# Up-projection of a gated feed-forward block by one level of Strassen's algorithm, with the down-projection as a stage of its own

## The chip, the core and the metric

The kernel runs on one core of a Trainium2 chip. The core has a matrix engine (TensorE, PE in the rows; PEld is its weight load), VectorE (DVE), ScalarE (ACT), GpSimd (POOL), and a queue engine SyncE (SP) that issues most transfers. Matmuls accumulate into eight PSUM banks; everything else lives in SBUF or, outside the core, in DRAM. The metric is the device time of one execution in microseconds, lower is better.

## What is computed

One decoder block on 1024 tokens of width 1024: two mixers (retention and sparse attention), a merge, an output projection, then a convolutional feed-forward block and a last norm. The change touches what follows the merge:

```python
x = x + merged @ w_out[l]
x = x + conv_ffn(rmsnorm(x, norm_ffn[l]), w_up[l], conv_w[l], conv_b[l], w_down[l])
...
def conv_ffn(h, w_up, conv_w, conv_b, w_down):
    a, b = jnp.split(h @ w_up, 2, axis=-1)          # w_up: 1024 x 5632
    a_pad = jnp.pad(a, ((0, 0), (CONV_W - 1, 0), (0, 0)))
    ac = conv_b + sum(conv_w[i] * a_pad[:, i:i + S] for i in range(CONV_W))
    return (jax.nn.gelu(ac) * b) @ w_down           # w_down: 2816 x 1024
```

All of it is wanted to float32 accuracy.

## The kernel before

**Split arithmetic.** Every operand of a matmul is kept as two tiles in the reduced float format that TensorE takes: `split` (line 128) writes the high part by a ScalarE copy and the low part by a VectorE subtraction that reads the high part. `mm3` (line 132) then makes three matmuls: high by high, high by low, low by high. One accumulation over 1024 input rows is 8 x 3 matmuls of 128 x 128 weights and 512 moving columns.

**Order.** Nobody wrote the order of the engines' instructions out by hand: the tile framework takes the program text as priority and a scheduler orders each engine's instructions. Every engine then runs its list strictly in that order, a transfer issue included, which waits in its engine's list like any other instruction. Tiles come from pools with a fixed number of buffers per tag: `wraw` (3, raw weights), `wsp` (4 per tag, `wh` and `wl`), `big` (4 of 16 KB per partition, tag `A`), `mpool` (12 of 8 KB, tag `B`), `fpool` (small rows). A new tile waits until the last reader of the buffer's former tile is done.

**Output projection** (from line 802). For each 512-column half `ch` and each token tile `t` of 128, eight k steps of `mm3` fill a bank `ps_mm`, and VectorE adds it to the residual row `x1[t]`, which stays in SBUF to the end. In the second half each tile is also normalised (`rms_row`: squares on ScalarE, power on GpSimd, scaling on VectorE), transposed by TensorE (eight 128 x 128 transposes) and split into `h2`, the moving operand of the up-projection (`hF`). Tiles go in the order 0 to 7.

**Up and down** (`up`, `down_weights`, `down`, from line 865). Features are taken in blocks `f` of 128. For a block and a token half `hf`, `up` makes two accumulations (the a and the b column block) of 24 matmuls, then ScalarE and VectorE do the convolution over tokens, Gelu, product and split; the gated rows `g2` stay in SBUF. Every two blocks `down` multiplies them by two rows of blocks of `w_down` and VectorE adds the sums to `x1`. Up of one pair and down of the pair before it alternate, and at the end the rows are normalised and stored.

Of the kernel before, what the change touches and what calls it, by code (L numbers as in the profile page):

```python
# [18 lines left out]
P = 128  # L19
# [65 lines left out]
def tile_hybrid_block(ctx: ExitStack, tc: tile.TileContext, x, norm_mix, w_in, ret_gn_g,  # L85
# [46 lines left out]
    def mm3(ps, ah, al, bh, bl, start, stop):  # L132
        nc.tensor.matmul(ps, ah, bh, start=start, stop=False)  # L133
        nc.tensor.matmul(ps, ah, bl, start=False, stop=False)  # L134
        return nc.tensor.matmul(ps, al, bh, start=False, stop=stop)  # L135
# [663 lines left out]

    x1 = [wsp.tile([P, D], F32, name=f"x1_{t}", tag="wh" if t < 4 else "wl") for t in range(NT)]  # L800
    hF = {}
    fpool = ctx.enter_context(tc.tile_pool(name="ftmp", bufs=1))
    gf = fpool.tile([P, D], F32, name="gf", tag="gain")
    nc.sync.dma_start(gf, bcast(norm_ffn[0], D))
    wo1 = [big.tile([P, KD, 512], F32R, name=f"wo1{i}", tag="A") for i in range(2)]

    def rms_row(t, gain, dst=None):
        hx = fpool.tile([P, D], F32, name="hx", tag="ft", bufs=3)
        ss = fpool.tile([P, 3], F32, name="ss", bufs=2)
        for i in range(2):  # L810
            c = slice(i * 512, i * 512 + 512)
            nc.scalar.activation(hx[:, c], x1[t][:, c], AF.Square, accum_out=ss[:, i:i + 1])
# [3 lines left out]
        for i in range(2):  # L816
            c = slice(i * 512, i * 512 + 512)
            nc.vector.scalar_tensor_tensor(hx[:, c], x1[t][:, c], r, gain[:, c],
# [4 lines left out]

    for t in range(NT):
        nc.sync.dma_start(x1[t], x[t * P:(t + 1) * P, :])
    for ch in range(2):
        cs = slice(ch * 512, ch * 512 + 512)
        for t in range(NT):
# [12 lines left out]
            if j == 0:  # L841
                hq = [half_quad("h2") for _ in range(2)]
                for k in range(KD):
                    hF[k, hf] = tuple(q[:, k % 4, :] for q in hq[k // 4])
            hx = rms_row(t, gf)
            for i in range(2):
# [4 lines left out]
                split(hq[i][0][:, :, c], hq[i][1][:, :, c], pt)  # L851
# [10 lines left out]
    wu, arow, g2, wd = {}, {}, {}, {}  # L862

    def up(f, hf):

        if hf == 0:
            wt = big.tile([P, 2, 2, KD, P], F32R, name="wu", tag="A")
            for i, c0 in ((0, f * P), (1, DFF + f * P)):
                raw = wraw.tile([P, KD, P], F32, name="wu_raw", tag="raw")
                nc.sync.dma_start(raw, w_up[:, c0:c0 + P].rearrange("(k p) c -> p k c", p=P))  # L870
                wu[f, i] = (wt[:, i, 0], wt[:, i, 1])
                split(*wu[f, i], raw)
        ps = []
        for i in range(2):
# [52 lines left out]
    for f in range(0, NF, 2):  # L927
        fs = (f, f + 1)
        for i in fs:
            up(i, 0)  # L930
# [34 lines left out]
```

## Time and profile before

| | us |
|---|---|
| median of 3 runs (1823.77 to 4637.19) | 1824.64 |
| the profiled execution | 1826.17 |
| its span, first to last instruction | 1824.4 |
| TensorE busy in it | 1791.2 (98%) |
| VectorE / ScalarE / GpSimd busy | 994.0 / 716.8 / 87.5 |
| weight loads busy (beside matmuls) | 1528.3 (84%) |

The profile counts an engine as busy while one of its instructions runs; a matmul's duration overlaps the next one's, so that the step from start to start, not the duration, says how fast they go. "Idle before" is the time in which an engine waited ahead of an instruction, with what ended the wait behind the arrow. The granted clock is the share of TensorE's full clock (1.00 is the upper of its two levels, 2.4 GHz, 0.50 the lower, 1.2 GHz); over the whole span it is 0.996.

### The profile page before, as it was taken

Reading aid. Unit: us, or ns where it says so; the run is one execution under the profiler, and the core shown is the slowest. Engines: PE = TensorE matmul, PEld = TensorE weight load, DVE = VectorE, ACT = ScalarE, POOL = GpSimd, SP = SyncE. Lnnn points to the kernel's source line nnn. Section 1 sums busy time; section 2 is a strip of 40 time slices with the busy share of each in tenths; the row PEclk is TensorE's granted clock in tenths of the full one; section 3 lists DMA queues with packets and bytes.
Section 4 is the critical chain, followed back from the end, with each engine's and each line's share of the span. In section 5 each row is a group of like instructions: output and inputs, shape, how many; then the busy total and the mean of one; then the engine's idle time right before and its main releaser. Section 6 shows DMA issues by size and latency. Waiting matters only on the chain.

```text
span 1824.4 us, 24239 instructions
## 1 busy us (share of the span) xinstructions
PE 1791.2 (98%) x9401; PEld 1528.3 (84%) x9401; DVE 994.0 (54%) x2245; ACT 716.8 (39%) x1345; POOL 87.5 (5%) x94
## 2 busy tenths in 40 slices
PE   8999999999999999999998999999999999999998
PEld 7888888988889988989777888888888888888886
DVE  6537666666667835557354355454344444445346
ACT  5435555554556734445443234122122222222213
POOL 1000000000000011220022000000000000000000
PEclk9999999999999999999999999999999999999999
DMA  5342222122221252223676303121121021112002
GB/s 204 110 142 70 73 62 72 50 80 65 63 80 53 68 154 85 70 87 129 219 235 227 120 1 98 30 70 35 35 70 47 24 69 58 35 47 70 12 1 93
DMA packets 164003, 151.08 MB, mean 83 GB/s; under 512 B 7606, under 2 KB 137134, under 8 KB 163886
## 3 DMA queue, kind: packets, MB, share of 16 engines
q1 hardware_dynamic: 142926, 122.77, 22.2%
q10 hardware_dynamic: 20960, 26.75, 4.1%
q8 instruction: 74, 1.21, 0.3%
q14 instruction: 43, 0.35, 0.1%
HBM read 118.55 MB, written 30.93 MB: 82 GB/s over the span
## 4 chain that ended last, share of the span: by engine, by line
PE 88%; DMA 5%; DVE 3%; ACT 2%; issue 1%; POOL 0%; SPq 0%; DVEq 0%; ACTq 0%; POOLq 0%
PE ps_mm L133 16%; PE ps_mm L134 16%; PE ps_mm L135 16%; PE ps_sc L133 7%; PE ps_sc L134 7%; PE ps_sc L135 7%; PE ps_pt L509 3%; PE ps_pv L134 2%; PE ps_pv L133 2%; PE ps_pv L135 2%; PE ps_sc L396 2%; PE ps_sc L395 2%; PE ps_pv L516 2%; PE ps_pv L515 2%; DMA sga<-ga_scr 1%
## 5 line engine op out<-in xcount | busy, mean ns | idle before, releaser
L133 PE MATMUL ps_sc<-h2h,wu 128*128 128x512 f32 x528 | 205.7, 390 | 0.0
L135 PE MATMUL ps_sc<-h2h,wu 128*128 128x512 f32 x528 | 205.4, 389 | 0.0
L134 PE MATMUL ps_sc<-h2l,wu 128*128 128x512 f32 x528 | 205.4, 389 | 0.0
L133 PE MATMUL ps_mm<-hTh,w_hi 128*128 128x512 f32 x512 | 202.1, 395 | 2.4 <-DVE ql L130 2.0
L134 PE MATMUL ps_mm<-hTl,w_hi 128*128 128x512 f32 x512 | 201.9, 394 | 0.0
L135 PE MATMUL ps_mm<-hTh,w_lo 128*128 128x512 f32 x512 | 201.1, 393 | 0.0
L922 DVE TENSOR_TENSOR x<-ps_mm,x 128x512 f32<-128x512 f32 x176 | 120.6, 690 | 146.4 <-PE ps_mm L135 144.8
L133 PE MATMUL ps_mm<-w_hi,hTh 128*128 128x256 f32 (+1 forms) x576 | 167.0, 290 | 1.7 <-DVE kl L130 1.1
L135 PE MATMUL ps_mm<-w_hi,hTl 128*128 128x256 f32 (+1 forms) x576 | 167.2, 290 | 0.0
L134 PE MATMUL ps_mm<-w_lo,hTh 128*128 128x256 f32 (+1 forms) x576 | 166.8, 290 | 0.0
L130 DVE TENSOR_TENSOR w_lo<-w_raw,w_hi 128x1024 fp32r<-128x1024 f32 (+2 forms) x75 | 92.0, 1229 | 110.4 <-ACT w_hi L129 110.4
L133 PE MATMUL ps_mm<-wd,g 128*128 128x512 f32 x352 | 137.5, 391 | 0.7 <-DVE ms L156 0.7
L134 PE MATMUL ps_mm<-wd,g 128*128 128x512 f32 x352 | 137.0, 389 | 0.0
L135 PE MATMUL ps_mm<-wd,g 128*128 128x512 f32 x352 | 137.0, 389 | 0.0
L129 ACT ACTIVATE pth<-ps_pt 128x512 fp32r<-128x512 f32 x132 | 76.6, 593 | 107.3 <-PE ps_pt L509 106.4
L133 PEld LDWEIGHTS ps_sc<-h2h,wu 128*128 128x128 f32 x528 | 99.1, 188 | 20.6
L135 PEld LDWEIGHTS ps_sc<-h2h,wu 128*128 128x128 f32 x528 | 99.0, 188 | 20.6
L134 PEld LDWEIGHTS ps_sc<-h2l,wu 128*128 128x128 f32 x528 | 99.1, 188 | 20.4
L133 PEld LDWEIGHTS ps_mm<-hTh,w_hi 128*128 128x128 f32 x512 | 96.3, 188 | 22.0 <-DVE ql L130 2.4
L133 PEld LDWEIGHTS ps_mm<-w_hi,hTh 128*128 128x128 f32 x576 | 110.5, 192 | 3.4 <-DVE kl L130 1.3
L135 PEld LDWEIGHTS ps_mm<-hTh,w_lo 128*128 128x128 f32 x512 | 96.3, 188 | 18.8 <-DVE w_lo L130 0.3
L134 PEld LDWEIGHTS ps_mm<-hTl,w_hi 128*128 128x128 f32 x512 | 96.3, 188 | 18.1
(284 smaller groups left out, 3782.9 us busy)
## 6 DMA issues: line engine op xcount, KB each, us to landing
w_raw<-in_w_in SPq DMA_DIRECT2D x48, 512.0 KB, 3.9
wu_raw<-in_w_up SPq DMA_DIRECT2D x44, 512.0 KB, 3.8
wd_raw<-in_w_down SPq DMA_DIRECT2D x22, 512.0 KB, 3.5
xt<-in_x SPq DMA_DIRECT2D x8, 512.0 KB, 5.2
qr<-q_scr SPq DMA_DIRECT2D x64, 64.0 KB, 2.4
ga_scr<-ge ACTq DMA_DIRECT2D x16, 256.0 KB, 2.0
rg_scr<-ge ACTq DMA_DIRECT2D x16, 256.0 KB, 2.1
gb_scr<-ge ACTq DMA_DIRECT2D x16, 256.0 KB, 2.0
```

Of the source, the lines that this page charges most:

```text
L129: nc.scalar.activation(hi, src, AF.Copy)
L130: nc.vector.tensor_sub(lo, src, f32(hi))
L133: nc.tensor.matmul(ps, ah, bh, start=start, stop=False)
L134: nc.tensor.matmul(ps, ah, bl, start=False, stop=False)
L135: return nc.tensor.matmul(ps, al, bh, start=False, stop=stop)
L395: nc.tensor.matmul(dst, q1[:, r, :], kap, start=True, stop=False)
L396: nc.tensor.matmul(dst, q2[:, r, :], kap, start=False, stop=True)
L509: nc.tensor.transpose(pt[:, r, :], pr[r][:, kt * P:(kt + 1) * P], ident)
L515: nc.tensor.matmul(pv[0:DK], v[:, 0:DK], ptl, start=False, stop=False)
L516: nc.tensor.matmul(pv, v, pth, start=False, stop=last)
L922: nc.vector.tensor_add(x1[t][:, cs], ps, x1[t][:, cs])
```

## The change

The up-projection is done on 2 x 2 blocks with seven products in place of eight (Strassen's algorithm in Winograd's form). The normalised input is cut into token halves and input halves (a11, a12 for tokens 0 to 511, a21, a22 for the others; the second index is the half of the 1024 inputs), and a 256-column strip of `w_up` into b11 to b22 (first index: input half, second: 128-column block). The sums s1 = a21 + a22, s2 = s1 - a11, s3 = a11 - a21 and s4 = a12 - s2 are made once, on the fly, as tiles are normalised; for that the second half of the output projection takes tiles 4 to 7 first, then 0 to 3. For every strip the differences t1 = b12 - b11, t2 = b22 - t1, t3 = b22 - b12 and t4 = b21 - t2 are made by VectorE and split too. `seven` makes the seven products of one strip (4 k steps, 12 matmuls each) in three banks: `c` collects s1 t1 and then s4 b22, `xb` collects a11 b11, s2 t2, s3 t3 and a22 t4, `yb` holds a12 b21. Between two products into one bank the partial sum is copied out (`kept`) or read by the output step; `skip_group_check` only allows accumulation to go on after a read. The last product (a22 t4) of a strip is put off into the next strip.

The a strip of two blocks is followed by their b strip. Outputs are rows of 1024 tokens in the one buffer `rows`; the convolution works on 1024 tokens at a time. The gated rows go to DRAM (`g_scr`, 44 writes of 256 KB issued by ScalarE). x1 goes to DRAM as well (`x1_scr`) and its buffers are used for weights. Behind the whole up stage the down stage loads x1, the gated rows (22 loads of 512 KB) and `w_down`, splits both, and accumulates two, then five times four feature blocks per bank. The last norm is interleaved with the last chunk.

```diff
-        for t in range(NT):
+        for t in (range(NT) if ch == 0 else (4, 5, 6, 7, 0, 1, 2, 3)):
...
+            hx = rms_row(t, x1[t], gf)
+            nc.scalar.dma_start(x1_scr[t], x1[t])
...
-                split(hq[i][0][:, :, c], hq[i][1][:, :, c], pt)
+                if hf == 1:
+                    if i == 0:
+                        nc.scalar.activation(fa[:, 0, :, c], pt, AF.Copy)
+                    else:
+                        split(a22[0][:, :, c], a22[1][:, :, c], pt)
+                        nc.vector.tensor_add(fa[:, 1, :, c], pt, fa[:, 0, :, c])
+                        split(s1[0][:, :, c], s1[1][:, :, c], fa[:, 1, :, c])
+                elif i == 0:
+                    split(a11[0][:, :, c], a11[1][:, :, c], pt)
+                    nc.vector.tensor_sub(fa[:, 0, :, c], pt, fa[:, 0, :, c])
+                    nc.vector.tensor_sub(fa[:, 1, :, c], fa[:, 1, :, c], pt)
+                else:
+                    split(a12[0][:, :, c], a12[1][:, :, c], pt)
+                    nc.vector.tensor_sub(fb[:, :, c], pt, fa[:, 1, :, c])
...
+        nc.vector.tensor_sub(t12[:, 0], b12, b11)
+        nc.vector.tensor_sub(t12[:, 1], b22, t12[:, 0])
+        split(wt[:, 0, 0:2], wt[:, 1, 0:2], t12)
...
+    def product(ps, a, b, start, stop):
+        for k in range(4):
+            mm3(ps, b[0][:, k, :], b[1][:, k, :], a[0][:, k, :], a[1][:, k, :],
+                start and k == 0, stop and k == 3, not start)
...
+        c = bank("sc")
+        product(c, s1, t1, True, True)
+        m5 = kept(c, 0)
+        xb = bank("mm")
+        product(xb, a11, b11, True, True)
+        m1 = kept(xb, 1)
+        while late:
+            late.pop()()
+        yb = bank("pt")
+        product(yb, a12, b21, True, True)
+        out(0, yb, m1)
+        product(xb, s2, t2, False, True)
+        u2 = kept(xb, 1)
+        product(c, s4, b22, False, True)
+        out(1, c, u2)
+        product(xb, s3, t3, False, True)
+        out(3, xb, m5)
+        def last():
+            product(xb, a22, t4, False, True)
+            out(2, xb, None)
+        late.append(last)
...
+                nc.vector.tensor_add(in1, in0, in1)
+                nc.vector.tensor_mul(g, in1, g)
+            nc.scalar.dma_start(g_scr[f + i % 2][:, tok], g)
...
+            ws[f] = rows_split(f, "wd", w_down[f * P:(f + 1) * P, :], *(
+                (big, "A") if f < 2 else (mpool, "B")))
+            gs[f] = rows_split(f, "g", g_scr[f], *(
+                (big, "A") if f < 2 or f % 4 < 2 else (mpool, "B")))
```

The built orders at three places. First TensorE at the end of the output projection, before: `ps_mm` is the last token tile (7), `wo` and `m` its operands, `ps_sc` the first up-projection accumulation, of tokens 0 to 511.

```order
L134 MATMUL ps_mm_11199<-wo11_10601,mh_10252 128x512
L135 MATMUL ps_mm_11199<-wo10_10600,ml_10253 128x512
L133 MATMUL ps_sc_11268<-h2h_10860,wu_11259 128x512
L134 MATMUL ps_sc_11268<-h2l_10861,wu_11259 128x512
L135 MATMUL ps_sc_11268<-h2h_10860,wu_11259 128x512
```

The same place in the changed kernel: `ps_mm_11255` is token tile 3, the last one now; the L865 rows are the transposes of tiles 2 (`hx_11226`) and 3 (`hx_11281`); `ps_mm_11374` and `ps_mm_11484` are the a11 products of the first and the second strip.

```order
L135 MATMUL ps_mm_11255<-wo10_10600,ml_10251 128x512
L865 MATMUL ps_pt_11238<-ident_116,hx_11226 128x128 x4
L865 MATMUL ps_pt_11247<-ident_116,hx_11226 128x128 x4
L865 MATMUL ps_pt_11293<-ident_116,hx_11281 128x128 x4
L865 MATMUL ps_pt_11302<-ident_116,hx_11281 128x128 x4
L133 MATMUL ps_mm_11374<-a11h_11112,d11_11346 128x512
L133 MATMUL ps_mm_11484<-a11h_11112,d11_11456 128x512
L134 MATMUL ps_mm_11374<-a11l_11113,d11_11346 128x512
```

The first product moved behind the transposes of the last tile; before, products of the first token half stood directly behind the output projection, with the transposes of later tiles among them.

Second, VectorE at the norm of tile 3. Before, from the residual sum of tile 3 to that of tile 4:

```order
L835 TENSOR_TENSOR x1_3_10590<-ps_mm_10991,x1_3_10590 128x512
L813 TENSOR_TENSOR ss_11018<-ss_11018 128x1
L156 TENSOR_SCALAR ms_11023<-ss_11018 128x1
L818 SCALAR_TENSOR_TENSOR hx_11017<-x1_3_10590,r_11022,gf_10598 128x512 x2
L130 TENSOR_TENSOR h2l_10861<-ps_pt_10977,h2h_10860 128x4x128
L130 TENSOR_TENSOR h2l_10863<-ps_pt_10984,h2h_10862 128x4x128
L835 TENSOR_TENSOR x1_4_10591<-ps_mm_11042,x1_4_10591 128x512
```

In the changed kernel, from the small sum of squares of tile 3 (its residual sum stands six rows ahead, with `fb`, `t12`, `a11l` and two `fa` rows between) to the low part of a11 for this tile (`a11l` from `ps_pt_11293`):

```order
L821 TENSOR_TENSOR ss_11282<-ss_11282 128x1
L920 TENSOR_TENSOR t34_11340<-wu_raw_11337,wu_raw_11335 128x512
L921 TENSOR_TENSOR t34_11340<-wu_raw_11337,t12_11339 128x512
L130 TENSOR_TENSOR a12l_11115<-ps_pt_11247,a12h_11114 128x4x128
L881 TENSOR_TENSOR fb_10895<-ps_pt_11247,fa_10894 128x4x128
L156 TENSOR_SCALAR ms_11287<-ss_11282 128x1
L826 SCALAR_TENSOR_TENSOR hx_11281<-x1_3_10590,r_11286,gf_10598 128x512 x2
L130 TENSOR_TENSOR d21_11459<-wu_raw_11447,d21_11459 128x512
L130 TENSOR_TENSOR d22_11466<-wu_raw_11447,d22_11466 128x512
L130 TENSOR_TENSOR d11_11585<-wu_raw_11574,d11_11585 128x512
L130 TENSOR_TENSOR a11l_11113<-ps_pt_11293,a11h_11112 128x4x128
```

Between the norm's steps stand differences for the strips (`t34`), the a12 and s4 rows of tile 2 and the splits of plain weight blocks (`d21`, `d22`, `d11`).

Third, ScalarE near the end of the up stage. Before, around the last blocks: convolution (L890), Gelu (L896), gated rows (`g2`) and evictions (L882), with the splits of `w_down` among them.

```order
L882 ACTIVATE ar_15387<-ps_sc_15337 128x512
L890 ACTIVATE ac_15392<-ps_sc_15337,cw_11250 128x512
L129 ACTIVATE wd_15466<-wd_raw_15464 128x1024
L129 ACTIVATE wd_15471<-wd_raw_15469 128x1024
L896 ACTIVATE ac_15392<-ac_15392 128x512
L129 ACTIVATE g2_15325<-ac_15392 128x512
```

In the changed kernel, from the last output of the last a strip (L979) on: `wd` and `g` are tiles of the down stage, L989 and L995 the scaled copy and Gelu of the last pair, `m_13999` the u2 copy of the last strip.

```order
L979 ACTIVATE rows_11334<-ps_mm_13890 128x512
L129 ACTIVATE wd_14138<-wd_raw_14136 128x1024
L989 ACTIVATE rows_11334<-rows_11334,cw_11327 128x1024
L129 ACTIVATE g_14143<-g_raw_14141 128x1024
L995 ACTIVATE rows_11334<-rows_11334 128x1024
L1005 DMA g_scr20_10630<-rows_11334 128x512
L946 ACTIVATE m_13999<-ps_mm_14014 128x512
L129 ACTIVATE wd_14286<-wd_raw_14284 128x1024
L1005 DMA g_scr21_10631<-rows_11334 128x512 x2
L129 ACTIVATE g_14291<-g_raw_14289 128x1024
L129 ACTIVATE wd_14148<-wd_raw_14146 128x1024
L1005 DMA g_scr20_10630<-rows_11334 128x512
```

The split of the first gated row read back (`g_14143`) now stands between the scaled copy and the Gelu of the last pair, and the second one's weights and rows stand behind the last writes to `g_scr`.

## Rows read from the trace of the kernel before

**Rows 1.** Windows: us; busy (count) of PE, PEld, DVE, ACT, POOL; clock, DMA, GB/s.

```profile
1041.00:1094.60 53.60, 53.60 (x263) 44.82 (x262) 26.38 (x51) 15.46 (x38) 3.83 (x7) 1.00 0.08 24
1094.60:1798.00 703.40, 703.40 (x3113) 582.56 (x3112) 317.44 (x477) 177.43 (x249) 0.55 (x1) 1.00 0.15 45
```

**Rows 2.** Who waited, PE, 1040 to the end: us, times, longest.

```profile
PE ps_mm L133 <- DVE ms L156: 0.7, 1, 0.7
```

**Rows 3.** Timeline of PE: start us, us; the first and the twelfth after it.

```profile
1797.83 0.39 PE L133 MATMUL ps_mm<-wd,g 128*128 128x512 f32 x1
...
1800.55 0.39 PE L133 MATMUL ps_mm<-wd,g 128*128 128x512 f32 x1
```

**Rows 4.** Tiles h2h and wd: count, ns min/median/max, first and last start.

```profile
L133 PEld LDWEIGHTS ps_sc<-h2h,wu x528: 187/188/190, 1094.6 to 1786.7; 128*128 128x128 f32 x176
L135 PE MATMUL ps_mm<-wd,g x352: 387/389/397, 1140.7 to 1816.4; 128*128 128x512 f32 x176
```

**Rows 5.** Groups by shape, DVE: count, busy us, mean ns, idle before.

```profile
L130 DVE TENSOR_TENSOR wu<-wu_raw,wu 128x1024 fp32r<-128x1024 f32 x44 | 53.9, 1225 | 75.6 <-ACT wu L129 75.6
...
L130 DVE TENSOR_TENSOR g<-ac,g 128x512 fp32r<-128x512 f32 x44 | 30.2, 686 | 1.4 <-ACT g L129 1.4
...
L207 DVE SCALAR_TENSOR_TENSOR hx<-xt,r,gm 128x1024 f32<-128x1024 f32 x8 | 10.2, 1281 | 1.4 <-POOL r L157 1.4
```

**Rows 6.** Groups by shape, ACT.

```profile
L129 ACT ACTIVATE wu<-wu_raw 128x1024 fp32r<-128x1024 f32 x44 | 46.7, 1061 | 140.7 <-DMA wu_raw<-in_w_up 130.2 <-PE ps_mm L135 6.9 <-PE ps_sc L135 1.9
...
L890 ACT ACTIVATE ac<-ps_sc,cw 128x512 f32<-128x512 f32 x44 | 34.0, 774 | 0.0
...
L882 ACT ACTIVATE ar<-ps_sc 128x512 f32<-128x512 f32 x44 | 26.3, 599 | 179.4 <-PE ps_sc L135 179.2
```

**Rows 7.** DMA issues of the page: count, KB, us to landing.

```profile
wu_raw<-in_w_up SPq DMA_DIRECT2D x44, 512.0 KB, 3.8
...
ga_scr<-ge ACTq DMA_DIRECT2D x16, 256.0 KB, 2.0
```

**Rows 8.** Timeline of DVE, norm of tile 7 behind the output projection.

```profile
1097.00 0.15 DVE L813 TENSOR_TENSOR ss<-ss 128x1 f32<-128x1 f32 x1
1097.19 0.15 DVE L156 TENSOR_SCALAR ms<-ss 128x1 f32<-128x1 f32 x1
1098.07 1.41 DVE L818 SCALAR_TENSOR_TENSOR hx<-x,r,gf 128x512 f32<-128x512 f32 x2 [0.73 <-POOL r L157]
1099.40 1.28 DVE L130 TENSOR_TENSOR h2l<-ps_pt,h2h 128x512 fp32r<-128x512 f32 x2
```

**Rows 9.** Timeline of PE, transposes of one normalised tile.

```profile
1058.99 1.04 PE L849 MATMUL ps_pt<-ident,hx 128*128 128x128 f32 x8
```

**Rows 10.** Timeline of PE behind two holes.

```profile
875.75 0.50 PE L133 MATMUL ps_mm<-oh,w_hi 128*128 128x512 f32 x1 [1.97 <-ACT yb L595]
...
1004.42 0.80 PE L133 MATMUL ps_mm<-woh,mh 128*128 128x512 f32 x1 [4.69 <-ACT mh L129]
...
1006.72 0.63 PE L133 MATMUL ps_mm<-woh,mh 128*128 128x512 f32 x1
1007.15 0.63 PE L134 MATMUL ps_mm<-wol,mh 128*128 128x512 f32 x1
...
1010.43 0.40 PE L133 MATMUL ps_mm<-woh,mh 128*128 128x512 f32 x1
```

**Rows 11.** Windows of 2 us behind those holes.

```profile
876.00:878.00 2.00, 2.00 (x8) 1.59 (x8) 1.69 (x2) 1.21 (x2) 0.00 (x0) 0.79 0.62 196
878.00:880.00 2.00, 2.00 (x6) 1.54 (x6) 1.22 (x1) 0.97 (x2) 0.00 (x0) 0.50 0.89 265
880.00:882.00 2.00, 2.00 (x9) 1.65 (x8) 0.16 (x1) 1.25 (x2) 0.00 (x0) 0.86 0.80 254
...
1008.00:1010.00 2.00, 2.00 (x6) 1.61 (x5) 2.00 (x3) 0.72 (x2) 0.00 (x0) 0.50 0.21 68
```

More of the change, by code (lines that the diff above doesn't have):

```diff
@@ L130, in split, with mm3 @@
         nc.vector.tensor_sub(lo, src, f32(hi))
[L132 to L135, printed above, removed]
+    def mm3(ps, ah, al, bh, bl, start, stop, more=False):
+        nc.tensor.matmul(ps, ah, bh, start=start, stop=False, skip_group_check=more)
+        nc.tensor.matmul(ps, ah, bl, start=False, stop=False, skip_group_check=more)
+        return nc.tensor.matmul(ps, al, bh, start=False, stop=stop, skip_group_check=more)
     def bcast(ap1d, n):
@@ L822, in rms_row, with block_pair @@
         return hx
+    def block_pair(name):
+        return [mpool.tile([P, 4, 512], F32R, name=name + i, tag="B") for i in "hl"]
     for t in range(NT):
@@ L840, in tile_hybrid_block @@
                 continue
[L841 to L845, printed above, removed]
+            if t == 4:
+                a22, s1 = block_pair("a22"), block_pair("s1")
+                fa = big.tile([P, 2, 4, 512], F32, name="fa", tag="A")
+                fb = big.tile([P, 4, 512], F32, name="fb", tag="A")
+            if t == 0:
+                a11, a12 = block_pair("a11"), block_pair("a12")
+            hx = rms_row(t, x1[t], gf)
+            nc.scalar.dma_start(x1_scr[t], x1[t])
+            pts = []
             for i in range(2):
@@ new lines, in tile_hybrid_block, with seven, kept @@
+    rows = big.tile([P, 2, 2, S], F32, name="rows", tag="A")
+    T0, T1 = slice(0, 512), slice(512, S)
+    late = []
+    def product(ps, a, b, start, stop):
+        for k in range(4):
+            mm3(ps, b[0][:, k, :], b[1][:, k, :], a[0][:, k, :], a[1][:, k, :],
+                start and k == 0, stop and k == 3, not start)
+    def seven(c0, out):
+        (t1, t2, t3, t4), (b11, b21, b22) = up_weights(c0)
+        m = fpool.tile([P, 2, 512], F32, name="m", tag="ft", bufs=4)
+        def kept(ps, i):
+            nc.scalar.activation(m[:, i], ps, AF.Copy)
+            return m[:, i]
+        c = bank("sc")
[19 more added lines that the diff above has]
+        late.append(last)
@@ new lines, in tile_hybrid_block, with rows_split @@
+    for f in range(0, NF, 2):
+        up(f)
+    while late:
+        late.pop()()
+    x1 = [wsp.tile([P, D], F32, name=f"x1_{t}", tag="wh" if t < 4 else "wl") for t in range(NT)]
+    for t in range(NT):
+        nc.sync.dma_start(x1[t], x1_scr[t])
+    gfin = fpool.tile([P, D], F32, name="gfin", tag="ft", bufs=4)
+    nc.sync.dma_start(gfin, bcast(norm_final, D))
+    def rows_split(f, name, src, pl, tag):
+        raw = wraw.tile([P, D], F32, name=name + "_raw", tag="raw")
+        nc.sync.dma_start(raw, src)
+        t = pl.tile([P, 2, D], F32R, name=name, tag=tag)
+        split(t[:, 0], t[:, 1], raw)
+        return t[:, 0], t[:, 1]
```

154 lines of the change are left out of this document (79 added, 75 removed).

## The prediction, made before the changed kernel ran

> **What bounds the kernel now.** I read the busy time by window first, then who waited for whom, then single rows. From the first up-projection matmul to 1798 us TensorE is busy for 703.40 of 703.40 us at clock 1.00, VectorE for 317.44 and ScalarE for 177.43; in the output projection ahead of it (1041.00 to 1094.60) it is busy for all 53.60 us [rows 1]. From 1040 us to the end TensorE's matmuls waited once for another engine, 0.7 us [rows 2]. So in these stages only the number of matmuls, and any new hole in their stream, sets the time. "Busy" can hide overlap, so I take the spacing: thirteen successive starts span 1797.83 to 1800.55, that is 12 steps of 0.2267 us [rows 3], although one row lasts 0.39. The stretch has 22 x 96 = 2112 up and 3 x 352 = 1056 down matmuls, each with its weight load, and 3168 x 0.2267 = 718.1 us; from 1094.6 to the end of the last step (1816.4 + 0.23) are 722.0 us [rows 4]. The 3.9 us left over are transposes and small holes near the end.
>
> **What is removed.** For each pair of 128-column blocks, a and b halves, the old code makes 2 x 2 x 8 x 3 = 96 matmuls and the new one 7 x 4 x 3 = 84. There are 22 such sets: 264 matmuls fewer, 264 x 0.2267 = **59.8 us**. The down-projection keeps its 1056. So 2904 matmuls remain, 658.3 us.
>
> The Trainium skill (TensorE: Matmul & The Clock Gate, Back-to-back issue gap) puts a sustained stream of weight load and 512-column matmul at about 131 ns each. By that figure the removed matmuls would be worth an estimated 34.6 us. The rows say 0.2267, and 3168 matmuls at 131 ns would fill only 415 of the 722 us that they took; the row decides.
>
> **What is added, in the steady state.** Per set VectorE gets four differences, two lo splits of 1024 columns and three of 512, and either three sums plus half of a convolution on 1024-wide rows or seven sums and products. With 0.69 for 512 columns, 1.23 for 1024, 1.28 for a scalar-tensor-tensor of 1024 [rows 5] a pair of sets costs 8 x 0.69 + 2 x (2 x 1.23 + 3 x 0.69) + 3 x 0.69 + 4 x 1.28 + 7 x 0.69 = 26.6 us. ScalarE: hi splits 2 x (2 x 1.06 + 3 x 0.60), seven evictions of 0.60, two scaled copies of 1024 (the 512 wide one takes 0.17 more than a plain copy, so some 1.3) and two Gelus (taken as copies, 1.1) make 17 us [rows 6]. TensorE takes 168 x 0.2267 = 38.1 us for the pair, so neither is the bound by sum. But seven products share three accumulators, and the new code copies or reads an accumulator before TensorE adds the next product to it. I walked one pair of sets along the built orders with these durations. The closest points: a new transformed weight tile waits for the last product of the set two earlier, then needs ScalarE (1.06) and VectorE (1.23), against 24 matmuls (5.4 us) that stand between; an accumulator's copy (0.60) has 10 to 24 matmuls, 2.3 to 5.4 us; the copy u2 in a b set waits behind convolution, Gelu and product and comes about 3 us ahead of its use. Weight loads of 512 KB land in 3.8 us, gated-row writes in 2.0 [rows 7], both with more room than that. The 44 write issues stand in ScalarE's queue and wait there for VectorE's products, with the next accumulator copy behind them; the walk counts that. So I take **nothing** here; the bound on the other side is a rival below. What hides this work is precisely those 2.3 to 5.4 us of other products; where they are gone, the chain of 3 to 8 us shows in full.
>
> **The start of the up stage.** Here no cover is left. Before, the rows 0 to 3 were normalised first, and products on them filled TensorE while rows 4 to 7 went through. Now the first product needs a11 of all four tiles 0 to 3, and these come last: in TensorE's order only 16 transposes stand between the last output-projection matmul (E) and a11. VectorE's order is long there. Between the sum x1_2 and the sum x1_3 stand 8 operations of 512 columns at 0.64 back to back, the small norm steps (0.15 + 0.15), a 0.73 us wait for GpSimd's power and 1.41 for the scaling [rows 8], with half a microsecond of waiting for transposes: 8.1 us, where TensorE needs 24 x 0.2267 + 0.9 = 6.3 (eight transposes: [rows 9]). VectorE is thus 1.8 us late at E. From there: sum 0.64, thirteen operations of 512 columns 8.3, norm 0.3 + 0.73 + 1.41, in all 13.2. ScalarE's a11 copy of tile 3 stands behind a weight split that waits for a load landing 3.8 us after its buffer is free; I add 0.5. So TensorE starts at E + **13.7 us** (11.4 without the lateness and the load; 16 if loads and the x1 writes slow each other).
>
> After it the clock. After a hole of 4.69 us matmuls stepped 0.43 us instead of 0.2267 from 1004.42 to 1010.43, at a granted clock of 0.50, the lower of its two levels; that is 14 matmuls, 14 x 0.20 = 2.8 us lost. After one of 1.97 us the clock stood at 0.79, 0.50 and 0.86 in three stretches of 2 us, 1.7 us lost [rows 10, 11]. The hole here is longer than both, so **2.8 us**. Behind that, four products that need no transformed weights (10.9 us and the 2.8) cover the splits of s2, s3, s4 and of t1 to t4: VectorE has the first pair at about E + 25.5, TensorE asks for it at E + 27. No more there.
>
> **The seam between up and down.** The last set has no following set to fill its waits. Let T be the end of the last product of the a set. ScalarE then does an eviction (0.60), a wd split (1.06), the scaled copy (1.3) and the g_14143 split, which waits for the buffer of s4, free at T + 5.4; only then the Gelu (to T + 7.7), VectorE's g split and product (T + 8.6) and the copy u2 (T + 9.3). TensorE's next product of the set could start at T + 6.1: 3.2 us lost. The following one waits for a VectorE sum behind others: 1.0. Then the first down group needs its fourth tile, in the buffer of the gated rows, free only when the last write has landed: product 0.69, issue, 2.0 [rows 7], splits 1.06 and 1.23, less 0.9 of cover: 4.4. Together 8.6; a half-clock spell after it, between the 1.7 and 2.8 of the two measured, 2.0: **10.6 us** (4.4 if the orders slip kindly and the clock holds, 14 if every load is late).
>
> **The down stage.** Splits of g anew (22 x 1.06 and 22 x 1.23) lie beside 1056 matmuls, 239 us. Sums of 0.69 each have 1.36 us per group in the first chunk and 2.7 later. Tiles 4 and 5 reuse buffers of tiles 0 and 1, so the second chunk's g starts when the first ends: about 1 us after cover of two half groups. With one more for first-chunk sums behind splits: **2 us** (0 to 5). x1 through DRAM: eight writes of 512 KB issued by ScalarE some 420 us ahead of the reads; the eight reads stand in SyncE's queue ahead of the second g load and behind buffers that are free by T + 5.4, and that load is wanted at about T + 18; nothing.
>
> **Sum.** From E: 13.7 + 2.8 + 658.3 + 10.6 + 2 = 687.4 against 722.0, 34.6 less. The profiled execution lasted 1826.2 us (span 1824.4), so 1791.6; the median of the runs shown is 1824.6, 1.5 lower. I forecast **1791 us**, 1.8% less.
>
> **Rivals.**
> *Cheaper seams.* With the lower ends above (11.4, no clock spell, 4.4, 0) the sum is 674.1: 1777 in terms of the median. For it: several pieces are in-order waits that a slightly different timing removes. Against: each of the two chains is a count of instructions that the built order fixes.
> *Small holes in every set.* 0.5 to 1.0 us per set, x 22: 1802 to 1813. For it: my walk leaves only some 3 us of room. Against: the old up stage, with its own chains from TensorE over ScalarE and VectorE, had not one hole.
> *The transformed weights become the bound* (the other side). If the eviction, the scaled copy, two scalar-tensor-tensors and the Gelu stand ahead of the split, the chain from a freed weight tile is 0.6 + 1.3 + 2.6 + 1.1 + 1.06 + 1.23 = 7.9 us or more against 5.4 of cover; with queueing some 3 us per set, 66 us: 1857. It ends above the old time from 34 / 22 = 1.5 us per set on. For it: two weight tiles only. Against: the order puts most splits ahead of the convolution.
> *Matmuls worth less.* Were the removed matmuls worth 34.6 us instead of 59.8, the sum gives 1816. The evenly spaced starts exclude that almost wholly. The Trainium skill's figure above is what this rival would rest on.
> That the matmuls are not removed is out: TensorE's built order has 2904 matmuls behind the transposes where the old one has 3168.
>
> **Chances.** Forecast (1783 to 1800) 0.60, cheaper seams 0.13, small holes 0.20, weights bound 0.06, matmuls worth less 0.01. Range: from 1779, inside the cheap seams, to 1811, which takes in most of the small holes. Faster by over 2% (about what a measurement here can tell from no change) means below 1788.1: the cheap seams and a third of the forecast case, 0.33. Slower by over 2%, above 1861: half of the weights case, 0.03. Within: 0.64.
>
> **What would show it.** A TensorE hole of 12 to 16 us behind the last output-projection matmul ending on a VectorE a11 split, followed by clock 0.50 for some 6 us; sets of 19.05 us each without holes, 84 starts at 0.2267; holes at the seam ending on a u2 copy and on the split of g behind a write to DRAM; the down stage at full step. The forecast is wrong if sets take 20 us or more, or if the first hole is under 10 us.

## The result, and the profile of the changed kernel

The changed kernel takes **1795.51 us** (median of four runs, 1794.92 to 1798.96) where the kernel before took 1824.54 beside it: a ratio of 0.9846 (95% interval 0.9827 to 0.9866), 1.5% less. One run of the kernel before was slow (4637 us) and is left out of the ratio. The forecast was 1791, range 1779 to 1811. The profiled execution lasted 1795.4 us (span 1793.6), 30.8 less than the one of before; the forecast in the same terms was 34.6 less.

Windows of the changed kernel, columns as in [rows 1]: the output projection, the up stage from its first product to the first wait near its end, the seam, the first part of the down stage, the rest of it.

```profile
1041.00:1093.00 52.00, 52.00 (x254) 43.01 (x252) 31.67 (x60) 20.52 (x46) 3.84 (x7) 1.00 0.21 82
1106.31:1521.90 415.59, 415.59 (x1825) 343.86 (x1825) 272.48 (x349) 176.58 (x231) 0.00 (x0) 1.00 0.27 90
1521.90:1538.40 16.50, 9.97 (x31) 6.46 (x31) 8.78 (x12) 6.72 (x7) 0.00 (x0) 0.90 0.55 175
1538.40:1580.00 41.60, 36.23 (x144) 27.33 (x144) 28.19 (x33) 13.56 (x13) 0.00 (x0) 0.96 0.52 174
1580.00:1786.40 206.40, 206.27 (x908) 169.87 (x906) 93.13 (x130) 36.53 (x55) 3.83 (x7) 1.00 0.23 78
```

The up stage is full from end to end, as the stretch of before was [rows 1]. VectorE's work in it has grown from 0.45 to 0.66 of the time and still hides. What is lost lies in front of the up stage and behind it. Who waited for whom, TensorE from 1040 us to the end, against the one wait of 0.7 us of before [rows 2]:

```profile
PE ps_pt L865 <- DVE hx L826: 5.7, 1, 5.7
PE ps_mm L133 <- DVE x L1046: 5.2, 4, 2.3
PE ps_mm L133 <- ACT g L129: 3.3, 2, 2.2
PE ps_pt L865 <- DVE fb L881: 2.4, 1, 2.4
PE ps_mm L133 <- ACT a11h L129: 1.8, 1, 1.8
PE ps_mm L133 <- ACT m L946: 1.1, 1, 1.1
...
```

The bookkeeping used from here on: E is the end of the last output-projection matmul's step, and a stretch has lost what it is longer than 0.2267 us for each of its matmuls. E is 1093.11 here and 1094.79 in the kernel before. It moved between 1088.4 and 1096.9 over the runs below in which every engine has the same list of instructions ahead of it (all but e7 to e10), so it says nothing of an edit behind it, and stages are compared from E, not by the span. e8 and e10 change the order of tiles ahead of E; more of that is said with e8. Except for e9 and e10 every run below is a single one; e11, the changed kernel once more, shows how far a stage moves by itself, up to 1.9 us.

| loss in us | E to first product | up stage | seam and down stage | E to the end, all |
|---|---|---|---|---|
| kernel before | | | | 3.7 |
| changed kernel | 13.2 | 2.1 | 19.7 | 35.0 |
| e1 eight products | 13.2 | 2.3 | 20.9 | 36.4 |
| e2 six products | 13.1 | 2.0 | 19.0 | 34.1 |
| e3 splits three times | 13.0 | 5.4 | 15.1 | 33.4 |
| e4 five accumulators | 13.0 | 1.8 | 11.2 | 26.0 |
| e5 early buffers | 13.2 | 2.0 | 9.9 | 25.0 |
| e6 seven load buffers | 13.2 | 2.4 | 29.0 | 44.6 |
| e7 weights after rows | 10.7 | 2.0 | 24.6 | 37.3 |
| e8 tiles in order | 0.0 | 18.4 | 17.8 | 36.3 |
| e9 = e4 + e5 + e7 | 10.7 | 2.4 | 0.8 | 13.8 |
| e10 = e4 + e5, start reworked | 0.0 | 14.2 | 0.1 | 14.3 |
| e11 changed kernel again | 13.1 | 1.9 | 21.6 | 36.6 |
| e12 = e4 + e5 | 13.1 | 1.7 | 0.8 | 15.6 |

From E to the end of the last matmul's step the changed kernel takes 693.3 us (1786.45 - 1093.11), the kernel before 721.9 (1816.65 - 1094.79; the prediction's 722.0 counts from the weight load just ahead of the first product): 28.5 less. The other 2.3 of the 30.8 are an E that came 1.7 earlier and 0.6 behind the last matmul.

### The profile page after: what moved, and what is told of

The parts are those of the page before. It is cut to its first block, busy times and chain, and to the rows that moved or that the text cites. A ratio compares the mean times of both kernels' runs of the same rounds, so it can differ in the third digit from the quotient of the medians.

```text
span 1793.6 us, 24041 instructions
## 1 busy us (share of the span) xinstructions
PE 1743.1 (97%) x9137; PEld 1482.9 (83%) x9137; DVE 1072.0 (60%) x2275; ACT 768.6 (43%) x1388; POOL 88.4 (5%) x94
## 4 chain that ended last, share of the span: by engine, by line
PE 86%; DMA 6%; DVE 4%; ACT 2%; issue 1%; POOL 0%; SPq 0%; DVEq 0%; ACTq 0%; POOLq 0%
PE ps_mm L133 20%; PE ps_mm L134 20%; PE ps_mm L135 20%; PE ps_pt L509 3%; PE ps_sc L133 3%; PE ps_sc L135 3%; PE ps_sc L134 3%; PE ps_sc L396 2%; PE ps_sc L395 2%; PE ps_pv L516 2%; PE ps_pv L515 2%; DMA sga<-ga_scr 2%; PE ps_pt L134 1%; PE ps_pt L135 1%; PE ps_pt L133 1%; DMA wd_raw<-in_w_down 1%
## 5 line engine op out<-in xcount | busy, mean ns | idle before, releaser
L1046 DVE TENSOR_TENSOR x<-ps_mm,x 128x512 f32<-128x512 f32 x96 | 65.8, 689 | 96.0 <-PE ps_mm L135 96.0
L130 DVE TENSOR_TENSOR ptl<-ps_pt,pth 128x512 fp32r<-128x512 f32 x132 | 89.8, 688 | 39.1 <-ACT pth L129 38.8
L129 ACT ACTIVATE w_hi<-w_raw 128x1024 fp32r<-128x1024 f32 (+2 forms) x75 | 78.5, 1047 | 80.7 <-PE ps_mm L134 48.5
L135 PEld LDWEIGHTS ps_mm<-hTh,w_lo 128*128 128x128 f32 x512 | 96.7, 189 | 18.9 <-DVE w_lo L130 0.3
L135 PEld LDWEIGHTS ps_mm<-w_hi,hTl 128*128 128x128 f32 x576 | 110.1, 191 | 1.2 <-DVE hTl L130 0.2
L134 PEld LDWEIGHTS ps_mm<-w_lo,hTh 128*128 128x128 f32 x576 | 110.2, 191 | 1.0
L133 PEld LDWEIGHTS ps_mm<-wd,g 128*128 128x128 f32 x352 | 66.5, 189 | 28.0 <-DVE x L1046 9.3
L135 PEld LDWEIGHTS ps_mm<-wd,g 128*128 128x128 f32 x352 | 66.4, 189 | 15.6 <-DVE g L130 1.8
```

Source lines behind the costliest of these rows:

```text
L129: nc.scalar.activation(hi, src, AF.Copy)
L130: nc.vector.tensor_sub(lo, src, f32(hi))
L133: nc.tensor.matmul(ps, ah, bh, start=start, stop=False, skip_group_check=more)
L134: nc.tensor.matmul(ps, ah, bl, start=False, stop=False, skip_group_check=more)
L135: return nc.tensor.matmul(ps, al, bh, start=False, stop=stop, skip_group_check=more)
L1046: nc.vector.tensor_add(x1[t][:, cs], ps, x1[t][:, cs])
```

## The experiments

### The steady state: what a matmul is worth, and how much room there is

e1 adds a product to each set, e2 leaves one out, e3 makes one split three times:

```diff
 e1     product(yb, a12, b21, True, True)
+       product(yb, s2, t2, False, True)
 e2     product(c, s4, b22, False, True)
        out(1, c, u2)
-       product(xb, s3, t3, False, True)
 e3 -   split(wt[:, 0, 0:2], wt[:, 1, 0:2], t12)
+       for _ in range(3):
+           split(wt[:, 0, 0:2], wt[:, 1, 0:2], t12)
```

> Each set issues one product more (s2*t2 a second time, added into the accumulator of a12*b21, so the rows come out changed); all else is as in the changed kernel. It brings TensorE back to the 3168 matmuls of the kernel before, behind the same start, staging and seam. Theory (a matmul is worth its spacing of 0.2267 us, and the up stage has no hole): 264 x 0.2267 = 59.8 us more, span 1793.6 + 59.8 = 1853.4, and the up stage 475.4 us instead of 415.6. Rival, matmuls worth 0.131 us: 34.6 more, span 1828. Rival, the transformed weights are close to being the bound: less than 59.8 comes on top, since the eighth product would also cover waits that are there now; the changed kernel shows none, so this would have to be hidden in slower steps.

> The product s3*t3 is left out of every set (the rows come out changed), with the splits, sums and copies all kept. A set has 72 matmuls, 16.3 us. It tells how far the steady state is from its next bound. Theory (VectorE's 26.6 us a pair against 32.6, and closest chains 2.3 to 5.4 us under cover): most of 59.8 us is saved, span 1734 to 1745, with holes of at most half a us in a set, on accumulator copies or transformed weights. Rival (cover is used up already, the walk's 3 us are the truth): taking 2.7 us of cover from each set opens holes of 1 to 2.7 us a set, 22 to 59 us, and the span stays at 1756 to 1793.

> The split of t1 and t2 into the transformed-weight tile is made three times over in every set: 2 x (1.06 + 1.23) = 4.6 us more in the chain that starts when that tile comes free, 4.9 us more VectorE work for a pair of sets (26.6 to 31.5 of 38.1). Theory of the prediction (5.4 us of other products cover a chain of 2.3): 6.9 against 5.4 leaves 1.5 us or more open in each set, 33 us or more, span 1827 or above, holes that end on the split of the transformed weights. Rival (other products are ready often enough, so only the engines' sums count): no holes, span 1793.6 to 1800.

They took 1856.89, 1729.91 and 1797.53 us (before, beside them: 1822.11). Windows behind the first few us of the up stage, one of each run (e1, e2, e3), TensorE alone for e1 (us; busy, count; clock, DMA, GB/s) and all engines for the others:

```profile
1110.30:1582.00 471.70, 471.70 (x2082) 1.00 0.24 80
```

```profile
1105.30:1459.60 354.30, 354.30 (x1565) 293.24 (x1563) 266.41 (x343) 170.84 (x229) 0.00 (x0) 1.00 0.32 105
```

```profile
1128.00:1528.50 400.50, 400.50 (x1768) 331.31 (x1766) 304.75 (x374) 210.34 (x264) 0.00 (x0) 1.00 0.28 94
```

TensorE waits for nothing in any of the three. With eight products the stretch from the first product to the first wait at the seam is 475.64 us for 2088 matmuls, with seven 415.56 for 1824: 60.1 for 264, 0.228 each. Leaving a product out gives 264 steps back in full: 632.6 us from E to the end against 693.3. The 4.6 us more that e3 puts in the chain of the transformed weights open no hole in the steady state, only one of 2.2 us right behind the start. So the first theory of e1 and e2 holds, and in e3 the rival does. (e2's span of 1728.1 even lies below the 1734 to 1745 that its theory gave: all of the 59.8 us came back, and its E was 4.7 us earlier.) The cover in e3 is wider than the 2.3 to 5.4 us of my walk, because the order is another one: the scheduler laid out a11 b11 and a12 b21 of a set, 24 matmuls that need no transformed weights, ahead of its s1 t1 in e3. VectorE's share went to 0.76 in e3 and 0.75 in e2 without a hole.

e1 also undoes Strassen's saving with everything else kept: 1856.9 against 1822.1 of the kernel before. The new staging alone costs about 35 us; the seven products give back 61.

### The seam and the down stage

Rows of the changed kernel's TensorE at the seam; the timeline shows start, duration and, in brackets, the wait ahead and who ended it.

```profile
1526.04 0.50 PE L133 MATMUL ps_mm<-s3h,wt 128*128 128x512 f32 x1 [1.10 <-ACT m L946]
...
1538.40 0.50 PE L133 MATMUL ps_mm<-wd,g 128*128 128x512 f32 x1 [2.19 <-ACT g L129]
...
1542.70 0.50 PE L133 MATMUL ps_mm<-wd,g 128*128 128x512 f32 x1 [2.31 <-DVE x L1046]
...
1551.89 0.50 PE L133 MATMUL ps_mm<-wd,g 128*128 128x512 f32 x1 [1.81 <-DVE x L1046]
```

The loss up to 1538.40 is 9.7 us, behind it 10.0. The wait at 1538.40 is for the split of the first chunk's last tile, and that one waits for the write of gated rows whose buffer it takes, as the prediction had it:

```profile
1537.29 1.06 ACT L129 ACTIVATE g<-g_raw 128x1024 fp32r<-128x1024 f32 x1 [1.28 <-DMA g_scr<-rows]
```

The two long waits of the second part end on VectorE's sums, and VectorE and ScalarE show why the sums are late:

```profile
1540.82 1.23 DVE L130 TENSOR_TENSOR wd<-wd_raw,wd 128x1024 fp32r<-128x1024 f32 x1 [1.21 <-ACT wd L129]
1541.96 1.28 DVE L1046 TENSOR_TENSOR x<-ps_mm,x 128x512 f32<-128x512 f32 x2
```

```profile
1539.73 1.06 ACT L129 ACTIVATE wd<-wd_raw 128x1024 fp32r<-128x1024 f32 x1 [1.38 <-DMA wd_raw<-in_w_down]
```

Two sums stand behind a split that waits for ScalarE, which waits for a load; with two accumulators (`mm`) TensorE stops. The loads are late, as I read it, because two of the three load buffers hold tiles that can't be split yet: their own buffers are those of the last transformed weights and of `rows`. Three edits, each for one link of this chain: more accumulators (e4), earlier buffers (e5), more load buffers (e6).

```diff
 e4 -   ps = bank("mm")
+       ps = bank(("mm", "sc")[(2 * t + ch) % 5 > 1])
 e5 -   ws[f] = rows_split(..., *((big, "A") if f < 2 else (mpool, "B")))
-       gs[f] = rows_split(..., *((big, "A") if f < 2 or f % 4 < 2 else (mpool, "B")))
+       late_tiles = (big, "A") if f % 8 in (4, 5) else (mpool, "B")
+       ws[f] = rows_split(..., *late_tiles)
+       gs[f] = rows_split(..., *late_tiles)
 e6 -   raw = wraw.tile([P, D], F32, name=name + "_raw", tag="raw")
+       raw = (fpool.tile([P, D], F32, name=name + "_raw", tag="ft", bufs=4)
+              if name == "g" and f < 18 else
+              wraw.tile([P, D], F32, name=name + "_raw", tag="raw"))
...
```

> Only the down stage is changed: its groups take their accumulators in turn from five banks instead of two. In the changed kernel the seam and the down stage lose 19.7 us against 1080 matmuls of 0.2267: 9.7 up to the start of the first group's second row block (1538.40), 10.0 after. Theory A (the second part is TensorE waiting for an accumulator because VectorE's sums stand behind splits that wait for loads): holes that end on the x sums go, with the half-clock spell they bring: 10.0 falls to 2 to 4, span 1786 to 1788. Theory B (the loads of the second chunk are late by as much): the holes move to the splits of wd and g of the second chunk, and span stays within 2 us of 1793.6.

> Only the buffers of the down stage's tiles are changed: the first chunk's four tiles (wd and g of blocks 0 and 1) take buffers of the row blocks s1, a11 and a12, which the last set reads first, instead of those of the last transformed weights, s4 and the gated rows, which come free last; later chunks share the rest. Theory A (two of the three load buffers are held from T to 1535 and 1537 by tiles whose own buffers come free last, so the second chunk's loads go one at a time through the third): the first chunk is ready before the last set ends, its groups fill the hole in front of s3*t3 (3.5 us) and the 2.2 us in front of the second block is gone, the second chunk's splits are 6 to 8 us earlier and VectorE's sums stop waiting: 19.7 us at seam and down stage fall to 4 to 8, span 1778 to 1782. Theory B (the transfers themselves are the limit, 512 KB in 4.2 us, eight of them against 21.8 us of first-chunk matmuls): the seam loses its 5.7 us, the second chunk keeps waiting, 10 us stay, span 1787 to 1789.

> Only the loads of the down stage are changed: g comes in through four buffers of its own (those of the weight differences, free after the last set), wd keeps the three; the load of the last gain waits for the last chunk. The tiles keep their late buffers. Theory A (load buffers held by tiles that cannot be split yet make the second chunk late): the seam's 9.7 us stay, the second chunk's splits come earlier, 10.0 us after 1538 fall to 2 to 5, span 1786 to 1789. Theory B (VectorE's sums wait behind splits whatever the loads do): the holes on the x sums stay, span within 2 us of 1793.6.

They took 1783.97, 1784.76 and 1802.74 us. TensorE's waits from 1500 us on (us in total, times, longest), e4:

```profile
PE ps_mm L133 <- ACT g L129: 5.2, 2, 4.1
PE ps_mm L133 <- DVE m L1003: 1.5, 1, 1.5
PE ps_mm L133 <- DVE rows L1001: 0.8, 1, 0.8
PE ps_mm L133 <- ACT m L946: 0.5, 1, 0.5
```

e5:

```profile
PE ps_mm L133 <- DVE x L1045: 3.5, 3, 1.7
PE ps_mm L133 <- DVE rows L1001: 2.6, 1, 2.6
PE ps_mm L133 <- DVE m L1003: 0.3, 1, 0.3
PE ps_mm L133 <- ACT m L946: 0.2, 1, 0.2
```

The Trainium skill (Perfetto Trace Analysis, Matmuls) says that independent groups of matmuls should rotate through different PSUM banks, so that emptying one overlaps the next group; e4 is that rule, and the trace agrees: no wait for an x sum is left, and behind the wait for the first chunk's last tile (ACT g, 4.1) only 1.8 us are lost, at half clock: its theory A, with 19.7 falling to 11.2. In e5 the first chunk's groups stand among the last set's products, the waits for ACT g are gone and the one for the u2 copy is 0.2; x sums still cost 3.5. It ends at 9.9, a little above theory A's 4 to 8.

In e6 neither theory held: 29.0 us were lost. Two of its waits that are much shorter in the other runs, and what stands ahead of the u2 copy on ScalarE:

```profile
PE ps_mm L133 <- DVE m L1003: 4.3, 1, 4.3
PE ps_mm L133 <- ACT m L946: 3.6, 1, 3.6
```

```profile
1524.90 1.06 ACT L129 ACTIVATE g<-g_raw 128x1024 fp32r<-128x1024 f32 x1 [2.72 <-DMA g_raw<-g_scr]
...
1525.87 1.04 ACT L129 ACTIVATE wd<-wd_raw 128x1024 fp32r<-128x1024 f32 x1
1526.81 0.58 ACT L946 ACTIVATE m<-ps_mm 128x512 f32<-128x512 f32 x1
```

With buffers free earlier, the scheduler put more splits of the down stage ahead of the last set's own copies and sums. The first of them waited 2.72 us for its load, and the u2 copy behind it waited too; that the loads came later than the order had allowed for is my reading. The x sums still waited 5.0 us in it, so that the held load buffers alone made them late is not shown; e5 moves buffers and loads together.

> Five accumulators in the down stage and early buffers for its first chunk, without the edit at the start. With that edit beside them the two left 0.8 us at seam and down stage, where one alone left 11.2 and the other 9.9. If the two really make up the whole loss, 0 to 2 us stay here as well, and with the start's 15.3 the last matmul ends at E + 674 to 676; if the edit at the start had a hand in it (it changes the order all the way down), more than 5 us stay.

e12 took 1774.86 us. TensorE's waits from 1108 us to the end are a single row:

```profile
PE ps_mm L133 <- DVE x L1045: 0.5, 1, 0.5
```

Of the 19.7 us 0.8 stay. The two savings add up (8.5 + 9.8 of 18.9), which fits two causes. It doesn't prove them apart, because the scheduler also found another order: in e12 the first group of the down stage stands ahead of 70 of the up stage's matmuls, where the changed kernel, e4 and e5 had 24 left. The last set has a following stage to fill its waits.

### The start of the up stage

e7 keeps the order of tiles and issues the next sets' weight preparation later; e8 takes the tiles 0 to 7 in order, so that the first four products need no row of the last tile.

```diff
...
 e7 +   with ExitStack() as later:
+           if c0 in (P * 2, DFF):
+               later.enter_context(tc.issue_after(a12_hi.ins))
+               later.enter_context(tc.issue_after(a11_lo.ins))
            (t1, t2, t3, t4), (b11, b21, b22) = up_weights(c0)
 e8 -   for t in (range(NT) if ch == 0 else (4, 5, 6, 7, 0, 1, 2, 3)):
+       for t in range(NT):
...
+                   nc.vector.tensor_sub(fa[:, 1, :, c], pt, fa[:, 0, :, c])
+                   nc.vector.tensor_sub(fb[:, :, c], fb[:, :, c], fa[:, 1, :, c])
...
```

> Only the order at the start of the up stage is changed: the preparation of the second and third set's weights is issued behind the a11 and a12 splits of tile 3. In the changed kernel the first product starts 12.5 us after E; ScalarE's copy a11h of tile 3 stands behind three weight splits that wait for loads until 1105.15, while the transposes were done by about 1104. Theory (that copy waits for loads of weights that nobody needs yet): the first product starts at E + 10.3 to 10.8, and nothing is lost later, span 1791 to 1792. Rival (VectorE's chain up to the scaling of tile 3 ends late anyway, or the second set's weights are then late): span within 0.7 us of 1793.6, or a new hole between the second and third product.

> The second half of the output projection takes the row tiles 0 to 7 in order, the a21 and a22 tiles last, with the sums formed as s3 = a11 - a21, s2 = a22 - s3, s4 = a12 - s2, and the first products' accumulators in banks that are idle there. Then a11*b11 and a12*b21 of the first two sets, 48 matmuls, need only tiles 0 to 3 and untransformed weights, and stand in TensorE's order between the last output-projection matmul and the last transposes. Theory (the hole at the start is waiting for the last tile's rows; 48 x 0.2267 = 10.9 us of products fill it): the first product starts within 1 us of E, the 12.5 us and the half clock of 2.1 shrink to 3 to 6 us in all, span 1783 to 1787. Rival (the wait only moves: s1*t1 needs the last tile's rows, t1 and t2 need a buffer that is free at E, and VectorE has as much to do): a hole of 8 us or more ahead of the first s1*t1, span 1790 or above.

They took 1795.82 and 1791.62 us. ScalarE of the changed kernel ahead of its first product shows what e7 removes: the copy a11h of the last tile stands behind weight splits that wait for loads, while the last eight transposes started at 1102.61.

```profile
1102.86 1.15 ACT L129 ACTIVATE d<-wu_raw 128x512 fp32r<-128x512 f32 x2 [5.30 <-DMA wu_raw<-in_w_up]
1105.15 0.63 ACT L129 ACTIVATE d<-wu_raw 128x512 fp32r<-128x512 f32 x1 [1.14 <-DMA wu_raw<-in_w_up]
1105.68 0.58 ACT L129 ACTIVATE a11h<-ps_pt 128x512 fp32r<-128x512 f32 x1
```

In e7 the first product starts at E + 10.7 instead of 13.2, inside the expected 10.3 to 10.8. The span did not follow, because the 2.5 us less at the start met a seam that lost 24.6 instead of 19.7. The order there had changed, 400 us behind the edit: one wd split, which waits 4.34 us for its load, now stands ahead of the last g split of the first chunk. So the rival's span came out, for neither of its reasons. Some 2 of the 4.9 us can be the play that e11 shows. In e8 the products start at E, and the rival's hole is there, TensorE from E to 40 us behind it:

```profile
PE ps_mm L133 <- ACT wt L129: 8.6, 1, 8.6
PE ps_pt L864 <- DVE fa L872: 2.2, 2, 1.4
...
```

The first s1 t1 starts at E + 26.5 (1114.58 - 1088.08), about where the changed kernel has its own (1119.31, E + 26.2). VectorE is busy for 23.89 of the 26.42 us in between. So the hole was not the wait for one tile alone: VectorE's sums and splits stand ahead of s1 t1 in either order of tiles. That VectorE's work alone sets it is not shown, because the split of t1 also stands behind those of s2 and s4 in e8, which e10 turns round. e8's time is 3.9 us below the changed kernel's, though it lost 36.3 us against 35.0: its E was 5.0 us earlier. Counted from the first matmul of the output projection's second half, where its order of tiles begins to differ, the two take the same (742.7 and 742.6 us); the order in e8 makes that half 1.2 us shorter, in e10 1.1.

### Together

e9 puts the edits of e4, e5 and e7 together. e10 has those of e4, e5 and e8, the first set's weights ahead of the splits of s2, and:

```diff
 e10 +  veng = nc.gpsimd if c0 in (0, DFF) else nc.vector
...
-       nc.vector.tensor_sub(t12[:, 0], b12, b11)
+       veng.tensor_sub(t12[:, 0], b12, b11)
...
-       split(d11[:, 0], d11[:, 1], b11)
+       split(d11[:, 0], d11[:, 1], b11, veng)
...
```

> Three edits together: five accumulators in the down stage, the first chunk in buffers that come free early, and the second and third set's weights behind the rows of tile 3. Counted from the end E of the last output-projection matmul to the end of the last matmul, and less 0.2267 us for each of the 2904 matmuls, the changed kernel loses 35.0 us: 15.3 at the start, 19.7 at seam and down stage. Alone the five accumulators left 11.2 of the 19.7, the early buffers 9.9, the later weights 12.7 of the 15.3. Theory A (the accumulator holes and the buffer holes are two causes): both go, 5 to 6 us stay at seam and down stage, 18 in all, end at E + 676 to 677. With E between 1088 and 1097, as in the runs so far, that is 1772 to 1783 us, most likely 1778, 0.974 of the kernel before. Theory B (they are one cause, seen at two places): 9 to 10 us stay, 22 in all, and the time is 1782.

> The down stage as in the run beside it (five accumulators, early buffers). At the start the tiles in order 0 to 7, the first set's weights prepared ahead of the splits of s2, s3 and s4, the differences and the lo splits of the first a and b set's weights on GpSimd instead of VectorE (where 512 columns of a product took 1.47 us), and the second pair's weights behind the last tile's rows. With the tiles in order alone the first product started at E, but s1*t1 had to wait until E + 26.5 for VectorE, which was busy without a pause from before E; 18.4 us were lost. Theory (VectorE's work up to the split of s1 and t1 is the limit: 27 us there, 8 us less here): s1*t1 starts at about E + 19, a hole of 3 to 4 us ahead of it and one of 1 to 2 ahead of s2*t2, 10 to 11 us lost at the start with the transposes, 2 us less than in the run beside it. Rival (GpSimd's differences, 4 x 1.47 behind the last norm, are late, and the split of t1 holds up ScalarE's queue): s1*t1 not before E + 23, 14 us or more lost, slower than the run beside it by 1 us or more.

e9 takes **1772.81 us** (median of five), 0.9734 of the kernel before (0.972 to 0.9747), and e10 **1772.44** (of four), 0.973 (0.9716 to 0.9743). Both take 2.7% less than the kernel before, where the changed kernel takes 1.5% less; between the two there is no difference. e9 went as theory A had it, and further: 13.8 lost instead of 18. In e10 s1 t1 started at E + 21.3, between its two forecasts, and the start lost 14.2, as its rival said, but the run was no slower than e9; so the reworked start is worth nothing beyond e7's one edit. Part of why is in the last section.

> The changed kernel itself once more, to see how far its stages differ between two executions of one program. From E to the end of the last matmul it lost 35.0 us: 13.2 before the first product, 2.1 at half clock behind it, 0 in the rest of the up stage, 19.7 at seam and down stage. If these are waits in a fixed order, they come back within 1 us each, and only E (1093.1) moves, by up to 4 us, as it did in the other runs. If the seam depends on when transfers happen to land, the 19.7 may come back anywhere between 15 and 25, as in the runs with other orders.

e11 took 1797.38 us. The start came back as 13.1 and 1.9, the seam up to 1538.60 with the same waits, and the first wait for an x sum as 2.95 instead of 2.31 us: 21.6 for 19.7 in all, which is more than the 1 us that a fixed order was expected to allow. The waits are the same ones in the same order, with some 2 us of play; that it comes from when loads land is likely, not shown.

## Why the prediction was right, and where it was off

**Removed matmuls:** 264 x 0.2267 stood. e1 gives 0.228 for each. The rival by the Trainium skill's 131 ns (TensorE: Matmul & The Clock Gate, Back-to-back issue gap) is out: it would have made e1 34.6 us longer from E to the end than the changed kernel, and it was 61.3.

**Steady state:** nothing lost, as predicted, and the two rivals (small holes, transformed weights as the bound) did not occur. But the reason was too narrow. I took 2.3 to 5.4 us as all the cover there was; e2 took 2.7 us out of each set and e3 added 4.6 to the chain, and neither opened a hole there.

**Start:** 13.7 + 2.8 forecast, 13.2 + 2.1 measured, but the parts compensate, so that the sum is in part luck. The hole ended on ScalarE's copy a11h, not on VectorE's a11 split as I had written. I gave ScalarE's wait for the load 0.5 us; e7, which removes it with three VectorE splits, gains 2.5. VectorE's chain of 512-column operations went at 0.60 us a step, not 0.64, which was half of a row of two [rows 8]. The half-clock spell behind it was 4.0 us long instead of some 6. Windows at the three places where the clock fell, at the start and twice at the seam (the last three columns are clock, DMA share, GB/s):

```profile
1106.00:1110.00 4.00, 3.69 (x9) 2.78 (x10) 4.00 (x7) 2.42 (x4) 0.00 (x0) 0.50 0.00 0
1526.60:1530.20 3.60, 3.60 (x10) 2.81 (x9) 1.46 (x3) 1.06 (x1) 0.00 (x0) 0.53 0.63 242
1543.80:1547.40 3.60, 3.60 (x10) 2.61 (x9) 2.53 (x4) 1.06 (x1) 0.00 (x0) 0.53 0.71 239
```

**Seam:** 10.6 forecast, 9.7 measured. The chain to the u2 copy lost 3.5 us (3.2 forecast), the sum behind it 1.1 (1.0), the fourth tile with a wait that I had not seen 3.4 (4.4), half clock 1.6 (2.0).

**Down stage:** this step failed: 2 forecast (0 to 5), **10.0** measured. The term "with one more for first-chunk sums behind splits" is the one that was mis-sized. Four waits for x sums cost 5.9 us (5.2 as idle time in the rows, the rest in the steps just behind them), a second half-clock spell 1.6, restarts and single slow steps the other 2.5. I had compared durations, a sum of 0.69 with a group of 1.36, and not looked at what stands ahead of the sums in VectorE's list and which loads these wait for. I also looked for the eight x1 loads ahead of the second g load only, and not for the load buffers that tiles with late buffers hold. e4 shows the link to the accumulators; e12 shows that accumulators and buffers together take away nearly the whole loss, in an order of its own.

So the forecast's 687.4 us from E on became 693.3: 1.2 less lost than forecast at the start, 0.9 less at the seam, 8.0 more in the down stage. In the whole time the miss is smaller, by luck: E came 1.7 earlier, and the output projection's second half, where the change begins, had started 2.0 earlier already (at 1043.9 instead of 1045.8). The rival of cheaper seams (674.1 from E on) did not come either; it took the edits of e4 and e5 together to get there (673.9 in e12). The step from the profiled time to the median was also short by 1: 1791.6 less 1.5 is 1790, not 1791.

## What to carry to other kernels

Where a change splits an interleaved stage in two, cost the ends before the middle: here the middle took all the extra work that was tried, and both ends, with no neighbour to fill their waits, took back more than half of what the products saved. Give the first tiles of the next stage the buffers that the last stage frees first, and enough accumulators that a sum behind a late split stops nobody; then the next stage's matmuls fill the last one's holes. More load buffers alone can harm: in e6 more waiting work stood ahead of needed work, in lists that run in order.

## What the runs showed of the hardware

In e10 VectorE's operations took longer beside GpSimd's. GpSimd, two low parts and later a difference, and VectorE at the same times:

```profile
1103.09 3.96 POOL L130 TENSOR_TENSOR d<-wu_raw,d 128x512 fp32r<-128x512 f32 x2 [1.69 <-ACT d L129]
...
1111.27 1.60 POOL L901 TENSOR_TENSOR t<-wu_raw,t 128x512 f32<-128x512 f32 x1
```

```profile
1103.60 2.29 DVE L130 TENSOR_TENSOR wt<-t,wt 128x1024 fp32r<-128x1024 f32 x1
1105.81 0.68 DVE L130 TENSOR_TENSOR a22l<-ps_pt,a22h 128x512 fp32r<-128x512 f32 x1
1106.41 0.67 DVE L875 TENSOR_TENSOR fa<-ps_pt,fa 128x512 f32<-128x512 f32 x1
...
1111.82 1.60 DVE L877 TENSOR_TENSOR s1l<-fa,s1h 128x512 fp32r<-128x512 f32 x1
```

VectorE's part of the split of t3 and t4 took 2.29 us where it takes 1.22 alone, the low part of s1 1.60 instead of 0.69; both read two operands from SBUF. The operations that read one operand from PSUM kept their 0.67 to 0.68. The Trainium skill (SBUF — State Buffer, SBUF: two separate sides) says that a VectorE operation with two SBUF inputs and a GpSimd operation that reads SBUF lock each other out for a whole instruction; these rows fit that (GpSimd's row ends at 1112.87, the low part of s1 0.55 us later). So work moved to GpSimd ran beside VectorE's undisturbed only where VectorE read PSUM.

The second is of the schedule and not of the chip, how far an order reaches: with an edit of a few instructions at 1095 us (e7) another order came out at 1530, and 4.9 us more were lost there than in the changed kernel, 3.0 more than in e11. Beside the edits of e4 and e5 the same edit cost nothing there (0.8 lost in e9 and in e12). A change of one place has to be read stage by stage, from a common point, or its effect is lost in that of another.
